# A hybrid decoder layer on one core: the inverse's last step with two heads side by side in the array, convolutions with two column places

## The chip, the cores and the metric

The kernel runs on one core of a Trainium2 chip, in one launch. The metric is the device time of one execution in microseconds (us), compared between kernels that ran on the same chip.

## What is computed

One layer of a decoder trunk for 512 tokens of width 1024, all in float32: a SwiGLU feed-forward block, a hybrid mixer, a second SwiGLU block, a last RMSNorm. The mixer projects its input into twelve groups of columns and has two branches. HGRN2 (8 heads) is a gated linear recurrence in chunks. Gated DeltaNet (16 value heads on 8 query/key heads) runs its q, k and v columns through a causal convolution of four taps with SiLU, and then, by chunks, the delta rule:

```python
def causal_short_conv(x, w):
    xp = jnp.pad(x, ((0, 0), (K - 1, 0), (0, 0)))
    return sum(xp[:, j:j + S] * w[j] for j in range(K))
...
    A = jnp.where(strict, jnp.einsum('bhntk,bhnsk->bhnts', kb, k) * Lmat, 0.0)
    T = lax.linalg.triangular_solve(eye + A, eye, left_side=True, lower=True, unit_diagonal=True)
    u = jnp.matmul(T, v * beta[..., None])
    w = jnp.matmul(T, kb * jnp.exp(gam)[..., None])
```

The inverse T of the unit lower triangular matrix is what the name "inverse" means below. The two branches are projected, gated, added and projected once more.

## The kernel before

Feature rows lie on the 128 partitions and the 512 tokens along the free dimension. Every large product is made of three matmuls (`mm3`, lines 164 to 166): weights and activations are split into a high and a low part in the type fp32r, and high by high, low by high and high by low are added up in PSUM. A weight block of 128x512 comes by DMA into a buffer `raw`, is cast by ScalarE (ACT) to `whi` and subtracted by VectorE (DVE) to `wlo` (lines 159 and 160 in the feed-forward blocks, 1368 and 1370 in the mixer). The program has three stages: the first feed-forward block, the mixer, and the second feed-forward block.

**What sets the order in the mixer.** Some hundred small generators (one for each head, inverse, convolution and gate) are run by a class `Desk` while the program is built. A generator asks for an engine and a time that the author priced (`yield V(512)` on DVE, `A(256)` on ACT, `T_(.9)` for .9 us of TensorE (PE)), for places (`yield "get", "mm", 1`), or for events. `Desk.run` keeps a clock for each engine, takes the request that can start first (ties by rank, or by a fourth element that goes ahead of the rank), and writes the instructions in that order. On the chip each engine then works through its own queue in order, and waits where an operand isn't there. So a change of a price or of a number of places moves instructions on all engines.

**Places the change speaks of.** `mm` is two PSUM banks for the large products: `product` (line 1376 on) takes one for a product of 24 matmuls with tile `pmm` (0.69 us for each three), or one for half of a product in token order with tile `pnat` (two token blocks, 48 matmuls). The bank goes back when the result has been read. `ta` is six buffers of 128x512 in SBUF (`TA = 6`), asked for by convolutions, the gates (`tgate`, tile `tg`, line 1136; `branch`, tile `yh`), the reloaded operands of the last product (`og`) and the merged gates (`mg`).

**A convolution** (`conv`, lines 763 to 785) waits for three `ta` places, reads the bank into `ci` on DVE (line 769; the bank is free after that), makes `cy` with one ACT and three DVE instructions (lines 774 and 777), a tanh `th` on ACT (line 780), and the output on DVE (line 783). Then it gives the three places back. 32 of them run, at most five unfinished at a time.

**The inverse** (`g_inv`, lines 940 to 987) runs eight times, each for eight 128x128 blocks: two heads by four token blocks, index s = 4i + c for head i. POOL has inverted the 32x32 diagonal blocks before. Two levels double them, 32 to 64 and 64 to 128; each level has two steps on PE with copies to SBUF on ACT:

```python
pe.matmul(q[a, s * hh:(s + 1) * hh], n2[b, s, a], ut[b, s, b], start=True, stop=True)
```

is the first (line 968, tile `pq`, copied into `acc`, line 971), and the second (line 978) multiplies by the transposed inverse (`tp` or `t64`) and is copied into `ut` (line 982). At the level 32 the rows `a` are two groups (0 to 31 and 64 to 95), so that two matmuls lie at different places of the array; at the level 64 there is one group, partitions 64 to 127 in and 0 to 63 out in the first step, and 0 to 63 in and out in the second: the eight blocks follow one another in one corner of the array. A float32 matmul is two recorded instructions: eight matmuls are "x16".

**The recurrence** (`g_rec`) uses the inverse: tiles `pw`, `pks`, `pog`, with DVE steps between (lines 1030 to 1070). `g_n` makes the 128x128 products ahead of it and takes a power on POOL (line 840).

Of the kernel before, what the change touches and what calls it, by code (L numbers as in the profile page):

```python
# [369 lines left out]
def mixer(tc, mp, e):  # L370
# [11 lines left out]
    def v3(ap, a):  # L382
        return ap.rearrange("p (a b) -> p a b", a=a)
# [378 lines left out]

    def conv(k, i, pt, out, n):

        yield "get", "ta", 3
        yield *V(512), 1
        ci = ta("ci", (P, T + 32))[:, :T + 3]
        dve.memset(ci[:, :3], 0.0)
        dve.tensor_tensor(ci[:, 3:], pt, rbc, op=ALU.mult)
        D.put("mm")  # L770
        wc = [cs[:, C_CV + 4 * i + j:C_CV + 4 * i + j + 1] for j in range(4)]
        yield A(512)
        y = ta("cy")
        act.activation(y, ci[:, :T], AF.Copy, scale=wc[0])
        for j in range(1, 4):
            yield V(550)
            dve.scalar_tensor_tensor(y, ci[:, j:j + T], wc[j], y, op0=ALU.mult, op1=ALU.add)
        yield A(512)
        th = ta("th")
        act.activation(th, y, AF.Tanh, scale=0.5)  # L780
        a, b = (v3(th, n), v3(y, n)) if n else (th, y)
        yield V(512)
        dve.scalar_tensor_tensor(out, a, 1.0, b, op0=ALU.add, op1=ALU.mult)
        D.put("ta", 3)
        D.fire(k)

    def g_e(u, st):
# [36 lines left out]
    def g_n(u, st):  # L824
        yield "on", "decays", ("k", u), *([("N", u - 1)] if u else []), *([("K", u - 4), ("R", u - 4)] if u > 3 else []), \
            ("kn", u) if u < 3 else "more"
        kq = st["kq"] = G["kq"][u % 4]
        kn = st["kn"] = G["kn"][u % 4]
        sm = st["sm"] = places["sm"]("sm", (P, 8, 8))
        for i in range(2):  # L830
            D.start((4, u, i), norms(u, i, kq, kn, sm))
        yield "on", ("norm", u, 0)

        hs = slice(2 * u, 2 * u + 2)
        rk = sm[:, 1, 0:4]
        yield V(4)
        dve.tensor_scalar(rk, sm[:, 0, 0:4], 4.0 * EPS, None, op0=ALU.add)
        yield "lag", EASE
        yield "use", "POOL", 1.2
        pool.tensor_tensor(rk, rk, mhalf[:, :4], op=ALU.pow)  # L840
        yield "lag", EASE
        s8 = lambda i: v3(sm[:, i], NT)
        c2, c3, c1 = st["c2"], st["c3"], st["c1"] = s8(2), s8(3), s8(4)
        yield "use", "DVE", .8
        dve.scalar_tensor_tensor(c2, beta[:, :, hs], 1.0, bc(rk, 2), op0=ALU.mult, op1=ALU.mult)
        dve.scalar_tensor_tensor(c3, c2, -1.0, bc(rk, 2), op0=ALU.mult, op1=ALU.mult)
        dve.tensor_tensor(c1, c3, eg[:, :, hs], op=ALU.mult)
        dve.tensor_scalar(c2, c2, 0.5, None, op0=ALU.mult)
        D.fire(("C", u))
        yield "on", ("q", u)  # L850
        yield "on", ("qm", 0), ("n2", u % 2)
        yield "get", "gm", 1
        gm, qm = places["gm"]("gm", (P, NT, P)), G["qm"][0]
        for hf in range(2):
            yield "get", "e", 1
            yield T_(.88)
            pq = ps("pgq", "e")
            for c in (2 * hf, 2 * hf + 1):
                pe.matmul(pq[:, (c % 2) * 256:(c % 2) * 256 + 256], kq[:, c, 0],
                          kq[:, c].rearrange("p a b -> p (a b)"), start=True, stop=True)  # L860
            p4 = pq.rearrange("p (c a b) -> p c a b", c=2, a=2)
            yield V(256)
            dve.tensor_tensor(gm[:, 2 * hf:2 * hf + 2], p4[:, :, 0], mid(strict, 2), op=ALU.mult)
            yield V(256)
            dve.tensor_tensor(qm[:, 2 * hf:2 * hf + 2], p4[:, :, 1], mid(tri, 2), op=ALU.mult)
            D.put("e")
        yield "on", ("E", u), *([("I", u - 2)] if u > 1 else [])
        st["at"] = []
        n2 = st["n2"] = G["n2"][u % 2]
        for i in range(2):  # L870
            a = G["at"][u % 4 * 2 + i]
            for c in range(NT):
                yield V(150)
                dve.scalar_tensor_tensor(n2[:, i, c], gm[:, c], c3[:, c, i:i + 1], a[:, c], op0=ALU.mult, op1=ALU.mult)
        D.put("gm")
        D.start((3, u), g_b(u, st))
        for i in range(2):
            a = G["at"][u % 4 * 2 + i]
            yield V(512)
            dve.tensor_tensor(a, qm, a, op=ALU.mult)  # L880
            st["at"].append(a)
        D.fire(("N", u))
# [57 lines left out]
    def g_inv(u, st):  # L940
# [10 lines left out]
        for b in range(4):  # L951
            r = slice(32 * b, 32 * b + 32)
            yield V(256)
            dve.transpose(ut[r, :, r], tp[r])
        for b in range(2):
            r = slice(32 * b, 32 * b + 32)
            yield A(256)
            act.copy(t64[r, :, r], tp[r])
        for hh in (32, 64):
            yield "get", "d", 1  # L960
            yield T_(.9)
            q = ps("pq1")
            qs = e["acc"]
            rows = [slice(2 * hh * g, 2 * hh * g + hh) for g in range(64 // hh)]
            nxt = [slice(2 * hh * g + hh, 2 * hh * g + 2 * hh) for g in range(64 // hh)]
            for s in range(8):
                for a, b in zip(rows, nxt):
                    pe.matmul(q[a, s * hh:(s + 1) * hh], n2[b, s, a], ut[b, s, b], start=True, stop=True)
            for a in rows:
                yield A(8 * hh)  # L970
                act.copy(qs[a, :8 * hh], q[a, :8 * hh])
            D.put("d")
            yield "get", "d", 1
            yield T_(.9)
            q2 = ps("pq2")
            for s in range(8):
                for a, b in zip(rows, nxt):
                    pe.matmul(q2[a, s * hh:(s + 1) * hh], tp[a, s] if hh == 32 else t64[:, s],
                              qs[a, s * hh:(s + 1) * hh], start=True, stop=True)
            for a, b in zip(rows, nxt):  # L980
                yield A(8 * hh)
                act.copy(ut[a, :, b], v3(q2[a, :8 * hh], 8))
            D.put("d")
            if hh == 32:
                yield V(256)
                dve.transpose(t64[32:64, :, 0:32], ut[0:32, :, 32:64])
        D.fire(("I", u))

    def g_rec(u, st):
# [175 lines left out]
    def operand(k, wait, get, make):  # L1165
# [9 lines left out]
        yield "lag", LAG["raw"]  # L1175
        if k > 8:
            yield "on", "projected"
        yield A(512)
        a, b = so[k] = make()
        act.copy(a, og)  # L1180
        yield V(512)
        dve.tensor_tensor(b, og, a.bitcast(F32), op=ALU.subtract)
        D.put("ta")
        D.fire(("so", k))
# [292 lines left out]
                                ("we", "we", 1, col), ("w", "w", 1, col)):  # L1477
        D.start((6, 0), claim(name, tag, n, shape))
    D.start((6, 0), claim("ut", "ut", 1, (P, 8, P), True))
    D.start((6, 0), claim("t64", "t64", 2, (64, 8, 64), True))  # L1480
    D.start((6, 0), second())
    D.start((6, 0), more())
    for u in range(8):
# [102 lines left out]
```

## Time and profile before

| | us |
|---|---|
| median of three runs | 1673.5 |
| the three runs | 1672.55, 1673.5, 1675.9 |
| the profiled execution | 1673.15 |
| its span, first to last instruction | 1671.4 |
| PE busy | 1645.5 |
| DVE busy | 968.0 |
| ACT busy | 698.0 |
| POOL busy | 322.4 |

The profiled execution took 1673.15 us by the same clock as the runs; 1.75 us of it lie outside the span. PE is busy nearly all the time. Matmuls are pipelined: one of 128x512 is recorded with some 0.39 us, and the next starts 0.23 us later, so that the distance between starts, not the recorded duration, is what an instruction costs on a full PE. In rows of the timeline the first column is the start, the second the duration of the merged group, the last the number of instructions; in square brackets stands the idle time before it and what ended it. PE's shapes are rows*columns of the array that the weights take, and then the moving operand.

### The profile page before, as it was taken

The page shows a single profiled execution, that of the slowest core. Times are in us where ns is not written, and L with a number is a line of the kernel's source. Part 1 is how long each engine was busy: PE and PEld are TensorE (multiplying, and loading weights), DVE is VectorE, ACT ScalarE, POOL GpSimd, SP SyncE. Part 2 cuts the span into 40 slices and gives each one's busy share as a digit, 9 for nine tenths or more (in the row PEclk, how much of TensorE's full clock was granted, in tenths as well). Part 3 has the DMA queues.
Part 4 walks back from the last instruction along what each step waited for, and adds up shares of the span by engine and source line. Part 5 has one row for each costly group of instructions (what it writes and reads, how often), then busy time and mean ns, then how long its engine had stood idle before and what let it go on. Part 6 is the DMA issues. An engine that isn't in the chain of part 4 may idle for free. (4 is left out here: it accounts for less than half of the span.)

```text
span 1671.4 us, 27476 instructions
## 1 busy us (share of the span) xinstructions
PE 1645.5 (98%) x10130; PEld 1397.4 (84%) x10130; DVE 968.0 (58%) x1992; ACT 698.0 (42%) x1523; POOL 322.4 (19%) x637
## 2 busy tenths in 40 slices
PE   8999999999999999999999999999999999999997
PEld 6888888888888898888888888887888888888886
DVE  5544443337677777657877788755545444444233
ACT  5333332333334345446665565554324433333332
POOL 2000000001121221561532756600001000000001
PEclk9999999999999999999999999999999999999998
DMA  5233333432222222444334353355544233333333
GB/s 174 89 98 98 95 98 108 117 119 71 77 65 66 77 82 73 148 136 108 99 112 117 95 131 106 118 159 166 174 145 138 89 96 100 95 98 95 98 94 112
DMA packets 141223, 181.21 MB, mean 108 GB/s; under 512 B 53008, under 2 KB 58640, under 8 KB 141088
## 3 DMA queue, kind: packets, MB, share of 16 engines
q1 hardware_dynamic: 140272, 177.78, 35.8%
q8 instruction: 80, 1.31, 0.3%
q0 software_dynamic: 384, 1.05, 0.2%
q10 hardware_dynamic: 432, 0.62, 0.1%
q14 instruction: 55, 0.45, 0.1%
HBM read 163.11 MB, written 16.29 MB: 107 GB/s over the span
## 5 line engine op out<-in xcount | busy, mean ns | idle before, releaser
L164 PE MATMUL pmm<-uh,whi 128*128 128x512 f32 (+1 forms) x1280 | 515.9, 403 | 7.9 <-ACT whi L301 7.0
L166 PE MATMUL pmm<-uh,wlo 128*128 128x512 f32 (+1 forms) x1280 | 500.0, 391 | 0.0
L165 PE MATMUL pmm<-ul,whi 128*128 128x512 f32 (+1 forms) x1280 | 499.8, 390 | 0.0
L159 ACT CAST whi<-raw 128x512 fp32r<-128x512 f32 (+1 forms) x290 | 176.5, 609 | 404.7 <-PE pmm L165 383.9
L160 DVE TENSOR_TENSOR wlo<-raw,whi 128x512 fp32r<-128x512 f32 (+1 forms) x290 | 203.1, 702 | 243.6 <-ACT whi L159 243.6
L164 PEld LDWEIGHTS pmm<-uh,whi 128*128 128x128 f32 (+1 forms) x1280 | 240.5, 188 | 56.4 <-ACT whi L301 7.3
L166 PEld LDWEIGHTS pmm<-uh,wlo 128*128 128x128 f32 (+1 forms) x1280 | 240.2, 188 | 52.6 <-DVE wlo L302 0.5
L165 PEld LDWEIGHTS pmm<-ul,whi 128*128 128x128 f32 (+1 forms) x1280 | 240.8, 188 | 45.3
L1368 ACT CAST whi<-raw 128x512 fp32r<-128x512 f32 x241 | 149.1, 620 | 250.0 <-PE pmm L165 163.3
L1370 DVE TENSOR_TENSOR wlo<-raw,whi 128x512 fp32r<-128x512 f32 x241 | 168.8, 702 | 140.0 <-ACT whi L1368 137.4
L202 POOL TENSOR_TENSOR acc<-acc,sqt 128x512 f32<-128x512 f32 x24 | 32.4, 1351 | 799.9 <-ACT sqt L200 799.6
L164 PE MATMUL pnat<-whi,uh 128*128 128x256 f32 x512 | 155.0, 303 | 3.2 <-DVE ggz L1157 2.0
L166 PE MATMUL pnat<-whi,ul 128*128 128x256 f32 x512 | 145.3, 284 | 0.0
L165 PE MATMUL pnat<-wlo,uh 128*128 128x256 f32 x512 | 145.2, 284 | 0.0
L164 PE MATMUL pmm<-gh,whi 128*128 128x512 f32 (+1 forms) x374 | 141.0, 377 | 0.0
L166 PE MATMUL pmm<-gh,wlo 128*128 128x512 f32 (+1 forms) x374 | 140.9, 377 | 0.0
L165 PE MATMUL pmm<-gl,whi 128*128 128x512 f32 (+1 forms) x374 | 140.8, 377 | 0.0
L910 POOL TENSOR_TENSOR fm<-gfs,ft 128x60 f32<-128x60 f32 (+24 forms) x248 | 94.9, 383 | 96.5 <-DMA ft<-hmask 77.9
L911 POOL TENSOR_TENSOR ft<-ft,fm 128x60 f32<-128x60 f32 (+24 forms) x248 | 99.6, 402 | 19.4
L164 PEld LDWEIGHTS pnat<-whi,uh 128*128 128x128 f32 x512 | 98.4, 192 | 5.8 <-DVE ggz L1157 2.2
L165 PEld LDWEIGHTS pnat<-wlo,uh 128*128 128x128 f32 x512 | 98.6, 193 | 0.7
L166 PEld LDWEIGHTS pnat<-whi,ul 128*128 128x128 f32 x512 | 98.2, 192 | 0.0
(374 smaller groups left out, 2189.0 us busy)
## 6 DMA issues: line engine op xcount, KB each, us to landing
raw<-wt SPq DMA_DIRECT2D x128, 256.0 KB
raw<-w1b SPq DMA_DIRECT2D x88, 256.0 KB
raw<-w1a SPq DMA_DIRECT2D x86, 256.0 KB
raw<-wn SPq DMA_DIRECT2D x64, 256.0 KB
raw<-w2b SPq DMA_DIRECT2D x45, 256.0 KB
raw<-w2a SPq DMA_DIRECT2D x40, 256.0 KB
raw<-wbg SPq DMA_DIRECT2D x32, 256.0 KB
gb<-gtd SPq DMA_DIRECT2D x16, 256.0 KB
```

The source lines that it names most:

```text
L159: act.copy(hi[:, :f], raw[:, :f])
L160: dve.tensor_tensor(lo[:, :f], raw[:, :f], hi[:, :f].bitcast(F32), op=ALU.subtract)
L164: pe.matmul(pt, ah, bh, start=first, stop=False)
L165: pe.matmul(pt, ah, bl, start=False, stop=False)
L166: pe.matmul(pt, al, bh, start=False, stop=last)
L202: pool.tensor_tensor(acc, acc, s, op=ALU.add)
L910: pool.tensor_tensor(tv, bc(m[:, j + 1:, j], w), t[:, j:j + 1, :w].to_broadcast([P, n, w]), op=ALU.mult)
L911: pool.tensor_tensor(t[:, j + 1:, :w], t[:, j + 1:, :w], tv, op=ALU.add)
L1368: act.copy(hi, raw)
L1370: dve.tensor_tensor(lo, raw, hi.bitcast(F32), op=ALU.subtract)
```

## The change

The level 32 is written out as before (`level32`), with the price of a PE step at .65 instead of .9. At the level 64 (`level64`), the four blocks of the second head are put into the other half of the array's columns: the first step reads partitions 64 to 127 for all blocks and writes partitions 0 to 63 of `q` for the first head and 64 to 127 for the second; its copy to `acc` is one of 128x256 in place of one of 64x512. For the second step `t64` holds the second head on partitions 64 to 127 (shape 128x4x64 in place of 64x8x64), so each head has its own corner of the array; the result goes to `ut` in two copies of 64x256 in place of one of 64x512. The matmuls alternate between the heads. The price of a step is .6 instead of .9. To fill `t64`, ACT has four copies of 32x128 where there were two of 32x256, and DVE two transposes of 32x128 where there was one of 32x256. The two levels' matmuls are as many and as large as before.

A convolution asks for two `ta` places: its tanh is written over `ci`. Three further edits change ranks alone: the power on POOL (line 840), and the cast and the subtraction of a reloaded operand (`operand`, lines 1178 to 1182), go ahead of others that could start at the same time.

```diff
--- before.py
+++ after.py
@@ -762,7 +762,7 @@
 
     def conv(k, i, pt, out, n):
 
-        yield "get", "ta", 3
+        yield "get", "ta", 2
         yield *V(512), 1
         ci = ta("ci", (P, T + 32))[:, :T + 3]
         dve.memset(ci[:, :3], 0.0)
@@ -776,12 +776,12 @@
             yield V(550)
             dve.scalar_tensor_tensor(y, ci[:, j:j + T], wc[j], y, op0=ALU.mult, op1=ALU.add)
         yield A(512)
-        th = ta("th")
+        th = ci[:, :T]
         act.activation(th, y, AF.Tanh, scale=0.5)
         a, b = (v3(th, n), v3(y, n)) if n else (th, y)
         yield V(512)
         dve.scalar_tensor_tensor(out, a, 1.0, b, op0=ALU.add, op1=ALU.mult)
-        D.put("ta", 3)
+        D.put("ta", 2)
         D.fire(k)
 
     def g_e(u, st):
@@ -836,7 +836,7 @@
         yield V(4)
         dve.tensor_scalar(rk, sm[:, 0, 0:4], 4.0 * EPS, None, op0=ALU.add)
         yield "lag", EASE
-        yield "use", "POOL", 1.2
+        yield "use", "POOL", 1.2, 1
         pool.tensor_tensor(rk, rk, mhalf[:, :4], op=ALU.pow)
         yield "lag", EASE
         s8 = lambda i: v3(sm[:, i], NT)
@@ -952,38 +952,64 @@
             r = slice(32 * b, 32 * b + 32)
             yield V(256)
             dve.transpose(ut[r, :, r], tp[r])
+
         for b in range(2):
             r = slice(32 * b, 32 * b + 32)
-            yield A(256)
-            act.copy(t64[r, :, r], tp[r])
-        for hh in (32, 64):
+            for i in range(2):
+                yield A(128)
+                act.copy(t64[64 * i + 32 * b:64 * i + 32 * b + 32, :, r], tp[r, 4 * i:4 * i + 4])
+        qs = e["acc"]
+        lo, hi = slice(0, 64), slice(64, 128)
+
+        def level32():
+            rows, nxt = (slice(0, 32), slice(64, 96)), (slice(32, 64), slice(96, 128))
             yield "get", "d", 1
-            yield T_(.9)
+            yield T_(.65)
             q = ps("pq1")
-            qs = e["acc"]
-            rows = [slice(2 * hh * g, 2 * hh * g + hh) for g in range(64 // hh)]
-            nxt = [slice(2 * hh * g + hh, 2 * hh * g + 2 * hh) for g in range(64 // hh)]
             for s in range(8):
                 for a, b in zip(rows, nxt):
-                    pe.matmul(q[a, s * hh:(s + 1) * hh], n2[b, s, a], ut[b, s, b], start=True, stop=True)
+                    pe.matmul(q[a, s * 32:(s + 1) * 32], n2[b, s, a], ut[b, s, b], start=True, stop=True)
             for a in rows:
-                yield A(8 * hh)
-                act.copy(qs[a, :8 * hh], q[a, :8 * hh])
+                yield A(256)
+                act.copy(qs[a, :256], q[a, :256])
             D.put("d")
             yield "get", "d", 1
-            yield T_(.9)
+            yield T_(.65)
             q2 = ps("pq2")
             for s in range(8):
                 for a, b in zip(rows, nxt):
-                    pe.matmul(q2[a, s * hh:(s + 1) * hh], tp[a, s] if hh == 32 else t64[:, s],
-                              qs[a, s * hh:(s + 1) * hh], start=True, stop=True)
+                    pe.matmul(q2[a, s * 32:(s + 1) * 32], tp[a, s], qs[a, s * 32:(s + 1) * 32], start=True, stop=True)
             for a, b in zip(rows, nxt):
-                yield A(8 * hh)
-                act.copy(ut[a, :, b], v3(q2[a, :8 * hh], 8))
+                yield A(256)
+                act.copy(ut[a, :, b], v3(q2[a, :256], 8))
             D.put("d")
-            if hh == 32:
-                yield V(256)
-                dve.transpose(t64[32:64, :, 0:32], ut[0:32, :, 32:64])
+
+        def level64():
+
+            heads = [(4 * i + j, slice(64 * i, 64 * i + 64), slice(64 * j, 64 * j + 64)) for j in range(4) for i in range(2)]
+            yield "get", "d", 1
+            yield T_(.6)
+            q = ps("pq3")
+            for s, r, c in heads:
+                pe.matmul(q[r, c], n2[hi, s, lo], ut[hi, s, hi], start=True, stop=True)
+            yield A(256)
+            act.copy(qs[:, :256], q[:, :256])
+            D.put("d")
+            yield "get", "d", 1
+            yield T_(.6)
+            q2 = ps("pq4")
+            for s, r, c in heads:
+                pe.matmul(q2[r, c], t64[r, s % 4], qs[r, c], start=True, stop=True)
+            for i in range(2):
+                yield A(256)
+                act.copy(ut[lo, 4 * i:4 * i + 4, hi], v3(q2[64 * i:64 * i + 64, :256], 4))
+            D.put("d")
+
+        yield from level32()
+        for i in range(2):
+            yield V(128)
+            dve.transpose(t64[64 * i + 32:64 * i + 64, :, 0:32], ut[0:32, 4 * i:4 * i + 4, 32:64])
+        yield from level64()
         D.fire(("I", u))
 
     def g_rec(u, st):
@@ -1175,10 +1201,10 @@
         yield "lag", LAG["raw"]
         if k > 8:
             yield "on", "projected"
-        yield A(512)
+        yield *A(512), 1
         a, b = so[k] = make()
         act.copy(a, og)
-        yield V(512)
+        yield *V(512), 1
         dve.tensor_tensor(b, og, a.bitcast(F32), op=ALU.subtract)
         D.put("ta")
         D.fire(("so", k))
@@ -1477,7 +1503,7 @@
                                 ("we", "we", 1, col), ("w", "w", 1, col)):
         D.start((6, 0), claim(name, tag, n, shape))
     D.start((6, 0), claim("ut", "ut", 1, (P, 8, P), True))
-    D.start((6, 0), claim("t64", "t64", 2, (64, 8, 64), True))
+    D.start((6, 0), claim("t64", "t64", 2, (P, 4, 64), True))
     D.start((6, 0), second())
     D.start((6, 0), more())
     for u in range(8):
```

## The prediction

> **What bounds the kernel now.** I read the page first, then PE by stages, then the list of what PE waited for, and last the timeline around the places that the change touches. The page gives the span and the share of each engine:
>
> ```profile
> span 1671.4 us, 27476 instructions
> PE 1645.5 (98%) x10130; PEld 1397.4 (84%) x10130; DVE 968.0 (58%) x1992; ACT 698.0 (42%) x1523; POOL 322.4 (19%) x637
> ```
>
> PE is the bound, and no other engine comes near. The four stretches below are most of the first feed-forward block, the mixer up to the first place where the changed order differs, the rest of the mixer up to its last product, and what follows; the columns are the length and the busy time of PE, PEld, DVE, ACT and POOL, the granted clock, and the DMA.
>
> ```profile
> 20.00:355.00 335.00, 334.03 (x1485) 276.60 (x1485) 151.60 (x228) 116.73 (x192) 12.36 (x10) 1.00 0.34 102
> 355.00:649.00 294.00, 294.00 (x2891) 258.12 (x2890) 206.47 (x539) 113.98 (x265) 56.50 (x70) 1.00 0.26 79
> 649.00:1170.00 521.00, 513.59 (x3462) 442.99 (x3461) 378.79 (x867) 287.81 (x774) 226.97 (x530) 1.00 0.43 122
> 1170.00:1660.00 490.00, 488.79 (x2240) 408.06 (x2239) 216.56 (x336) 165.88 (x271) 18.85 (x17) 1.00 0.36 109
> ```
>
> All that the change can reach lies in the third row. There PE is idle for 521.00 - 513.59 = 7.4 us; DVE and ACT have more than 140 us to spare. So two things count: how long PE's own instructions take, and which of the 7.4 us of waits stay. The waits of that stretch, by what ended them (total, times, longest):
>
> ```profile
> PE pmm L164 <- DVE tg L1136: 2.3, 1, 2.3
> PE pnat L164 <- DVE ggz L1157: 2.0, 1, 2.0
> PE pnat L164 <- DVE ci L769: 1.2, 1, 1.2
> PE pks L1030 <- DVE s L1070: 1.1, 2, 0.6
> PE pw L1043 <- DVE gx L1034: 0.5, 1, 0.5
> PE ptv L934 <- DVE gqm L865: 0.3, 1, 0.3
> ```
>
> They add up to 7.4: the list is whole.
>
> **Part 1: the last step's matmuls, two heads at a time.** The timeline of PE around the first inverse: each step with the row that follows it.
>
> ```profile
> 728.70 0.69 PE L968 MATMUL pq<-gut,gn 32*32 32x32 f32 x32
> 729.32 0.50 PE L164 MATMUL pmm<-uh,whi 128*128 128x512 f32 x1
> ...
> 735.83 1.14 PE L968 MATMUL pq<-gut,gn 64*64 64x64 f32 x16
> 736.90 0.65 PE L813 MATMUL ptk<-sq,h 128*128 128x128 f32 x4
> ...
> 738.88 1.14 PE L978 MATMUL pq<-acc,gt 64*64 64x64 f32 x16
> 739.96 0.50 PE L164 MATMUL pmm<-uh,whi 128*128 128x512 f32 x1
> ```
>
> From its start to the next one's, a 64-wide step takes 1.07 and 1.08 us for 16 instructions in one corner; the 32-wide step takes 0.62 us for 32 instructions at two places of the array. Does work at two places run side by side? The HGRN2 heads show it apart from the width, in products over all 128 rows that land on one, two or four groups of columns (lines 648 and 634):
>
> ```profile
> 413.62 0.45 PE L648 MATMUL pl<-qp,ke 128*32 128x32 f32 x16
> 414.00 0.39 PE L164 MATMUL pnat<-whi,uh 128*128 128x256 f32 x1
> ...
> 416.70 0.68 PE L648 MATMUL pl<-qp,ke 128*64 128x64 f32 x8
> 417.31 0.39 PE L164 MATMUL pnat<-whi,uh 128*128 128x256 f32 x1
> ...
> 418.94 0.45 PE L634 MATMUL pl<-qp,ke 128*32 128x16 f32 x32
> 419.31 0.39 PE L164 MATMUL pnat<-whi,uh 128*128 128x256 f32 x1
> ```
>
> 32 instructions on four groups take 0.37 us and 16 on two groups 0.38: eight to each group in both. 16 to each group (the 32-wide step) take 0.62. So the time goes by the instructions of one group, and the groups run beside each other. Of 64-wide ones, eight in one group take 417.31 - 416.70 = 0.61 us. The changed step has eight in each of two groups: I take 0.61. Each inverse saves (1.07 - 0.61) + (1.08 - 0.61) = 0.93, and eight inverses **7.4 us**, all of it on the bound engine. Ends: nothing, if the two halves follow one another; and no more than 7.4, since no row shows eight such instructions in less.
>
> [...] Line 648 at 413.62 has all rows in common and still takes 0.38 for 16. [...]
>
> The copies around the steps change on ACT:
>
> ```order
> L1368 CAST whi<-raw 128x512
> L971 COPY acc<-pq_7490 64x512
> L816 COPY gkn<-ptk 128x512
> L820 ACTIVATE ptk,sm<-ptk 128x128 x4
> L982 COPY gut<-pq_7527 64x8x64
> ```
>
> That was ACT at the 64 level of the first inverse before; this is the same place in the changed kernel:
>
> ```order
> L1394 CAST whi<-raw 128x512
> L820 ACTIVATE ptk,sm<-ptk 128x128
> L996 COPY acc<-pq_7578 128x256
> L820 ACTIVATE ptk,sm<-ptk 128x128 x2
> L801 ACTIVATE gqm<-gb,gx 128x128 x2
> L1005 COPY gut<-pq_7607 64x4x64 x2
> ```
>
> The copy between the two steps has half the elements to a partition, the one behind them has become two. The copies of this kind before, shortest, median and longest in ns (32x256 at the low end, 64x512 at the high end):
>
> ```profile
> L971 ACT COPY acc<-pq x24: 343/364/583, 729.4 to 1112.2; 32x256 f32<-32x256 f32 x16, 64x512 f32<-64x512 f32 x8
> ```
>
> By it an inverse pays .36 for .58 ahead of the second step, 2 x .36 for .58 behind it, and two more short copies for `t64`, at most .36 each: at the worst +0.6 us on ACT, and two DVE transposes for one. ACT is free for 521.00 - 287.81 us, and PE has large products between the steps, so I take 0. Without that cover a late copy would hold PE by its own .36, at most 2.9 us for eight inverses.
>
> **Part 2: the banks that convolutions held.** The longest stall of the stretch is at 662.71:
>
> ```profile
> 653.73 0.39 PE L166 MATMUL pmm<-uh,wlo 128*128 128x512 f32 x1
> ...
> 660.45 0.28 PE L166 MATMUL pnat<-whi,ul 128*128 128x256 f32 x1
> 662.71 0.52 PE L164 MATMUL pnat<-whi,uh 128*128 128x256 f32 x1 [1.98 <-DVE ggz L1157]
> ```
>
> ```profile
> 665.88 0.68 DVE L769 TENSOR_TENSOR ci<-pmm,rbc 128x512 f32<-128x512 f32 x1
> ```
>
> A convolution's product is complete at 653.73, but DVE reads it only at 665.88: for 12 us one of the two banks is held, and the halves of the next product (`pnat`) share the other. PE has to wait until the gate (line 1157) has emptied it. Why so late stands in DVE's order, from the gates of the waiting product (`pnat_6536`) to that convolution (`pmm_6433`), before:
>
> ```order
> L1157 SCALAR_TENSOR_TENSOR ggz_5781<-thg_6613,pnat_6536 128x256
> L874 SCALAR_TENSOR_TENSOR gn2_5718<-gm_6501,sm_6308,gat_5542 128x128
> L1157 SCALAR_TENSOR_TENSOR ggz_5781<-thg_6618,pnat_6536 128x256
> L732 TENSOR_TENSOR hrho_6514<-hrho_6514,rcol_83 128x4
> L735 SCALAR_TENSOR_TENSOR hon_6515<-po_6385,hrho_6514,hg_5780 128x128 x4
> L874 SCALAR_TENSOR_TENSOR gn2_5718<-gm_6501,sm_6308,gat_5542 128x128
> L880 TENSOR_TENSOR gat_5541<-gqm_6386,gat_5541 128x512
> L880 TENSOR_TENSOR gat_5542<-gqm_6386,gat_5542 128x512
> L783 SCALAR_TENSOR_TENSOR h_70<-th_6573,cy_6450 128x4x128
> L768 MEMSET ci_6691 128x3
> L769 TENSOR_TENSOR ci_6691<-pmm_6433,rbc_74 128x512
> ```
>
> The read comes right behind line 783, with which an older convolution gives its three places back: two convolutions had all six. Now the same product is `pmm_6435`, and the gates are those of `pnat_6529`:
>
> ```order
> L777 SCALAR_TENSOR_TENSOR cy_6451<-ci_6356,cs_75,cy_6451 128x512
> L768 MEMSET ci_6536 128x3
> L769 TENSOR_TENSOR ci_6536<-pmm_6435,rbc_74 128x512
> L1396 TENSOR_TENSOR wlo_6526<-raw_6398,whi_6527 128x512
> L777 SCALAR_TENSOR_TENSOR cy_6451<-ci_6356,cs_75,cy_6451 128x512
> L777 SCALAR_TENSOR_TENSOR cy_6458<-ci_6432,cs_75,cy_6458 128x512
> L863 TENSOR_TENSOR gm_6509<-pgq_6555,sq_76 128x256
> L865 TENSOR_TENSOR gqm_6385<-pgq_6555,sq_76 128x256
> L783 SCALAR_TENSOR_TENSOR h_70<-ci_6356,cy_6451 128x4x128
> L777 SCALAR_TENSOR_TENSOR cy_6458<-ci_6432,cs_75,cy_6458 128x512 x2
> L732 TENSOR_TENSOR hrho_6468<-hrho_6468,rcol_83 128x4
> L735 SCALAR_TENSOR_TENSOR hon_6469<-po_6384,hrho_6468,hg_5780 128x128 x4
> ```
>
> Three convolutions are under way (`cy_6451`, `cy_6458` and the new `ci_6536`), and the bank is read ahead of everything that it stood behind. So the 1.98 us should go. They had a sequel, by the granted clock (the last figure but two):
>
> ```profile
> 660.00:665.00 5.00, 3.02 (x18) 2.81 (x17) 3.44 (x12) 2.74 (x7) 0.00 (x0) 0.78 0.01 3
> 665.00:670.00 5.00, 5.00 (x39) 5.00 (x39) 2.16 (x5) 1.76 (x4) 0.52 (x1) 0.88 0.17 28
> ```
>
> The clock was not full for a while after the wait: (0.22 + 0.12) x 5.00 = 1.7 us of PE's work were lost. It goes if the wait goes. The second stall of the kind is named after the convolution itself:
>
> ```profile
> 994.90 0.39 PE L164 MATMUL pnat<-whi,uh 128*128 128x256 f32 x1 [1.25 <-DVE ci L769]
> ```
>
> In the changed order convolutions' reads follow their products closely there too. Together 1.98 + 1.7 + 1.25 = **4.9 us**. Ends: nothing, if waits as long come up at other places of the new order; and 4.9 + 4.2 = 9.1 if the other waits of the list go as well (2.3 + 1.1 + 0.5 + 0.3 = 4.2).
>
> **Part 3: what is only moved.** The other waits, 4.2 us, I keep as they are. The recurrence's (lines 1030 and 1043) come from a chain of PE and DVE that the change doesn't shorten. The last,
>
> ```profile
> 1165.62 0.47 PE L164 MATMUL pmm<-sogb,whi 128*128 128x512 f32 x1 [2.26 <-DVE tg L1136]
> ```
>
> is a gate that gets a `ta` place late, after the last convolution; gates, reloaded operands and merged gates ask for as many places as before. The tanh over `ci` adds no wait: it needs `cy`, which the last reading of `ci` makes. The power's rank moves it in POOL's queue, among the solver's instructions of the 32x32 blocks; POOL is busy for 226.97 of 521.00 us, so I take 0. An inverse that came late would show as a wait of the recurrence, whose largest one here is 0.6. The number of DMAs stays, the SP queue issues them in another order, and the large products keep their number. In PE's order the runs of large products between other work are 248 before and 248 now, so no more switches between kinds of matmul are paid.
>
> **Sum.** 1673.15 - 7.4 - 4.9 = 1660.8 for an execution like the profiled one, which lies 0.35 below the median of the runs shown. I say **1661**; its own range is 1658 to 1664, by the 4.2 us of other waits going either way by some two thirds.
>
> **Rivals.**
>
> *The waits move.* 32 convolutions, 16 gates and eight inverses stand in another order, planned with prices. For it: the waits of before were in no plan either. Against: the two that I take away have one cause, which the order shows gone. Then only part 1 is left: 1673.15 - 7.4 = 1665.8.
>
> *One step of the two stays serial.* Part 1 gives 3.7: 1664.5. If both do, the change doesn't do what it says, and part 2 alone gives 1668.2. Against both: 0.37 us for 32 on four groups. For: no row has 64-wide halves.
>
> *All waits go*, since the steps' prices (.65 and .6) are now near what a step costs (0.62 and 0.61; before .9 against 0.62 and 1.07), so that the plan drifts less: 1673.15 - 7.4 - 9.1 = 1656.7.
>
> *Slower: convolutions crowd the gates out.* With three convolutions in six places nothing is left for a gate (`tg` or `yh`, 24 of them), whose product then holds a bank as the convolution did. One such hold costs what the one at 662.71 did, 1.98 + 1.7 = 3.7 us. To be slower than before by 0.2% (3.3 us, about what a measurement of this kernel can tell from no change) it takes 12.3 + 3.3 = 15.6 us, so it decides from the fifth hold on: 1660.8 + 5 x 3.7 = 1679.3. For it: the wait at 1165.62 is of this sort. Against: a gate needs one place where a convolution needs two at once.
>
> **How the numbers follow.** Forecast 0.55; the waits move 0.17; one step serial 0.09; both serial 0.04; all waits go 0.05; slower 0.08; within 0.2%, by part 1 or 2 and some new waits, 0.02. Faster by over 0.2%: 0.55 + 0.17 + 0.09 + 0.04 + 0.05 = 0.90. The range from 1656 to 1668 takes in all but both serial and what is slower or equal, 0.14.
>
> **What would show it.** [...] Part 2: no wait of PE for line 769 or for the gates of `pnat` (now line 1183) near 650 to 670, and a granted clock of 1.00 there. Part 3: PE's idle time from 649 to the end of the mixer, near 4.2. The prediction is wrong if that idle time is 7 or more, or if the steps keep their length.

## The result: no change that the measurement can tell

| | before | after |
|---|---|---|
| median of 20 runs each on one chip, us | 1674.35 | 1674.09 |
| lowest and highest | 1671.69 to 1675.9 | 1669.64 to 1677.36 |
| ratio, 95% interval | | 0.9999 [0.9992, 1.0005] |
| the profiled execution, us | 1673.15 | 1671.58 |
| its span, us | 1671.4 | 1669.8 |

The forecast was 1661 with a range from 1656 to 1668: the time lies above all of it. Of the three parts of the reasoning the first two hold as mechanisms, and the profile after shows it. The page first:

```profile
span 1669.8 us, 27534 instructions
PE 1640.4 (98%) x10130; PEld 1392.4 (83%) x10130; DVE 969.9 (58%) x2000; ACT 699.3 (42%) x1547; POOL 322.1 (19%) x637
```

PE's share is 98% as before, and its busy time is 5 us less. The steps of the first inverse at the level 64, each with the row behind it:

```profile
748.82 0.68 PE L994 MATMUL pq<-gut,gn 64*64 64x64 f32 x16
749.43 0.50 PE L164 MATMUL pmm<-uh,whi 128*128 128x512 f32 x1
...
751.02 0.68 PE L1002 MATMUL pq<-acc,gt 64*64 64x64 f32 x16
751.63 0.50 PE L164 MATMUL pmm<-uh,whi 128*128 128x512 f32 x1
```

From start to start both steps take 0.61 us, and so do all sixteen. **Part 1 came to the hundredth of a microsecond.** Next the stretch of the two held banks, and then the mixer as a whole, by stretches with the granted clock as the last figure but two:

```profile
660.00:665.00 5.00, 5.00 (x45) 5.00 (x44) 3.30 (x9) 3.79 (x9) 0.31 (x1) 1.00 0.01 3
665.00:670.00 5.00, 5.00 (x30) 4.39 (x29) 4.48 (x10) 2.89 (x6) 0.00 (x0) 1.00 0.49 152
```

```profile
649.00:1168.00 519.00, 508.20 (x3463) 437.56 (x3462) 381.39 (x874) 289.46 (x799) 226.49 (x530) 0.99 0.42 123
```

From 660 to 670 PE is now busy throughout at full clock: **part 2's waits went.** But over the mixer PE is idle for 519.00 - 508.20 = 10.8 us, where before it was 7.4 and the prediction had 4.2. What it waits for there (total, times, longest):

```profile
PE pq L971 <- DVE gut L954: 5.2, 2, 4.6
PE pmm L164 <- DVE tg L1162: 2.4, 1, 2.4
PE pog L1083 <- DVE x L1074: 1.7, 1, 1.7
PE pq L981 <- ACT acc L974: 1.5, 1, 1.5
```

No wait of this list names a convolution (line 769) or the gates of `pnat` (line 1183). Three of its four names were not on the list of before; the fourth, `tg`, was the last wait there. The largest one stands at the first inverse, at 736.78. On PE:

```profile
731.84 0.39 PE L166 MATMUL pmm<-uh,wlo 128*128 128x512 f32 x1
736.78 0.24 PE L971 MATMUL pq<-gut,gn 32*32 32x32 f32 x2 [4.56 <-DVE gut L954]
```

The product before it is finished, and the next instruction in PE's order is the inverse's. Its matmuls need the second and the fourth of four transposes of DVE (line 954). DVE:

```profile
729.53 0.43 DVE L954 STREAM_TRANSPOSE gut<-gtp 32x256 f32<-32x256 f32 x1
735.57 0.69 DVE L1396 TENSOR_TENSOR wlo<-raw,whi 128x512 fp32r<-128x512 f32 x1 [5.61 <-ACT whi L1394]
736.29 1.36 DVE L954 STREAM_TRANSPOSE gut<-gtp 32x256 f32<-32x256 f32 x3
```

One transpose is done at 729.53, the other three stand behind a subtraction for a large product, which waits 5.61 us for its cast on ACT. ACT:

```profile
726.88 0.62 ACT L1394 CAST whi<-raw 128x512 fp32r<-128x512 f32 x1 [2.99 <-DMA raw<-wt]
733.09 1.28 ACT L801 ACTIVATE x<-gb,gx 128x128 f32<-128x128 f32 x4 [5.59 <-DMA gb<-gtd]
...
734.94 0.60 ACT L1394 CAST whi<-raw 128x512 fp32r<-128x512 f32 x1
```

The cast stands behind four activations of another head, which wait 5.59 us for `gb`, a row of gates that a DMA spreads over all partitions (line 796). And SP, which issues the DMAs:

```profile
721.18 5.87 SPq L923 DMA_DIRECT2D gln<-nt  x4
727.14 0.51 SPq L1377 DMA_DIRECT2D raw<-wt  x1
727.76 0.38 SPq L1151 DMA_DIRECT2D md<-yh  x1
728.18 0.42 SPq L796 DMA_DIRECT2D gb<-gtd  x1
```

The load of `gb` is issued only at 728.18, behind four loads of the solver's results (`gln`) that hold SP for 5.87 us. So PE's 4.56 us come down a chain of four queues: SP, ACT, DVE, PE. In the kernel before no load of `gb` stood between 715 and 737, and DVE made all four transposes in one go:

```profile
726.44 1.81 DVE L954 STREAM_TRANSPOSE gut<-gtp 32x256 f32<-32x256 f32 x4
```

The wait at the mixer's end has the same form. SP issues the store of a gate, `td<-tg`, behind nine loads for the gates' merging, 4.8 us after the tanh that makes it was done (1142.11 on ACT), and DVE can't write the next `tg` into the place until that store is done; the product whose bank DVE is to read then stops PE:

```profile
1146.94 0.32 SPq L1151 DMA_DIRECT2D td<-tg  x1
```

```profile
1152.58 0.69 DVE L1162 TENSOR_TENSOR tg<-pmm,rbc 128x512 f32<-128x512 f32 x1 [5.64 <-DMA td<-tg]
```

```profile
1153.42 0.54 PE L164 MATMUL pmm<-uh,whi 128*128 128x512 f32 x1 [2.36 <-DVE tg L1162]
```

Both waits were followed by a stretch at half clock:

```profile
737.26:744.10 6.84, 6.40 (x42) 4.72 (x42) 6.14 (x11) 4.81 (x12) 5.94 (x12) 0.50 0.39 116
1153.68:1157.10 3.42, 3.42 (x9) 2.68 (x9) 3.30 (x8) 1.59 (x4) 0.00 (x0) 0.50 0.37 115
```

PE is busy in them for 6.40 + 3.42 = 9.8 us and does about half as much (its 128x512 matmuls start 0.43 us apart there, 0.23 elsewhere): some 4.9 us are lost, against 1.7 before. The ledger of the span: 7.4 saved by the steps; 10.8 - 7.4 = 3.4 more of waits; 4.9 - 1.7 = 3.2 more lost to the clock. That is -0.8; the span moved by -1.6.

### The profile page after: what moved, and what is told of

Read it like the earlier page. It is cut to its first block, busy times and chain, and to the rows that moved or that the text cites. A ratio compares the mean times of both kernels' runs of the same rounds, so it can differ in the third digit from the quotient of the medians.

```text
span 1669.8 us, 27534 instructions
## 1 busy us (share of the span) xinstructions
PE 1640.4 (98%) x10130; PEld 1392.4 (83%) x10130; DVE 969.9 (58%) x2000; ACT 699.3 (42%) x1547; POOL 322.1 (19%) x637
## 5 line engine op out<-in xcount | busy, mean ns | idle before, releaser
L164 PE MATMUL pmm<-uh,whi 128*128 128x512 f32 (+1 forms) x1280 | 516.4, 404 | 10.2 <-ACT whi L301 6.9
L911 POOL TENSOR_TENSOR ft<-ft,fm 128x60 f32<-128x60 f32 (+24 forms) x248 | 99.3, 400 | 19.4
```

The source lines that it names most:

```text
L164: pe.matmul(pt, ah, bh, start=first, stop=False)
L911: pool.tensor_tensor(t[:, j + 1:, :w], t[:, j + 1:, :w], tv, op=ALU.add)
```

## The experiments

The theory after the two profiles: the steps save their 7.4 us, and the new order, which prices, places and ranks set together, gives them back in waits and in the slow clock behind them, above all through SP's queue. The rivals: the shorter steps aren't paid, because PE then waits for what it had met in time before, in any order; or one edit does it by itself, the two places or the ranks. The letters in the texts on record are those of each text.

Eleven kernels ran, in three groups; in each group the kernel before ran on the same chip (1674.71 us for experiments 1 to 4, 1675.08 for 5 to 8, 1675.0 for 9 to 11). All compute the whole layer.

**1. Only the new steps.** Before's order, prices, ranks and three places; only the level 64 is placed as in the change, in the same place of the order.

```diff
-                pe.matmul(q[a, s * hh:(s + 1) * hh], n2[b, s, a], ut[b, s, b], start=True, stop=True)
+                for s, r, c in heads:
+                    pe.matmul(q[r, c], n2[hi, s, lo], ut[hi, s, hi], start=True, stop=True)
...
+                    pe.matmul(q2[r, c], t64[r, s % 4], qs[r, c], start=True, stop=True)
```

> Part 1 alone: the order, the prices and the three places of the kernel before are kept, row by row on PE; only the 64 level's placement, its copies and the transposes are the changed kernel's. Theory A (the matmuls' saving is real and the new order gives it back in waits): 16 steps save 0.46 us each and the waits stay at the 7.4 us of before, so 1674.4 - 7.4 = 1667.0, ratio 0.9956. Rival B (the saving doesn't reach the end because something else than PE paces the mixer): 1674, ratio 1.000.

Measured: 1670.94 us, ratio 0.9983 [0.9975, 0.9991], between the two numbers of the text. Its steps take 0.61 us too, so 7.4 us left PE's work; 3.8 of them arrived by the medians, 2.8 by the ratio. In the profiled run PE's waits in the mixer grew from 7.4 to 11.6 us, though PE's instructions stand in the same order, one for one. One example, in the kernel before:

```profile
968.94 0.41 DVE L865 TENSOR_TENSOR gqm<-pgq,sq 128x256 f32<-128x256 f32 x1
```

```profile
969.72 0.81 PE L859 MATMUL pgq<-h 128*128 128x256 f32 x3
```

and in this kernel:

```profile
968.17 0.41 DVE L865 TENSOR_TENSOR gqm<-pgq,sq 128x256 f32<-128x256 f32 x1
```

```profile
968.73 0.89 PE L859 MATMUL pgq<-h 128*128 128x256 f32 x3 [1.73 <-DVE gqm L865]
```

Line 865 empties the tile that PE's next instruction writes. Before, DVE was done with it just before PE came (968.94 + 0.41 = 969.35 against 969.72). PE now comes earlier, DVE by only 0.77 us, and PE waits 1.73. DVE has hardly a gap there: the "140 us to spare" of the prediction are a mean over the mixer, and here it is DVE's queue that ends last. So a saving on PE is paid out only where the other engines are ahead by more than the saving.

**2. Only two places for a convolution.**

```diff
-        yield "get", "ta", 3
+        yield "get", "ta", 2
...
-        th = ta("th")
+        th = ci[:, :T]
...
-        D.put("ta", 3)
+        D.put("ta", 2)
```

> Part 2 alone: the kernel before with two places to a convolution and the tanh over ci, all else as it was; the order is planned anew. Theory A as in the prediction (the waits at 662 and 994 go, nothing else comes): 1674.4 - 4.9 = 1669.5, ratio 0.997. Theory A with new waits, as the changed kernel has them: between 1670 and 1678, and the wait for line 769 is gone all the same. Rival B: 1674, ratio 1.000.

Measured: 1689.9 us, ratio 1.0097 [1.0084, 1.011]: the edit that part 2 valued at -4.9 costs 15 us by itself. All three times of the text missed; that the waits for line 769 go was right. Its waits:

```profile
PE pto L1103 <- DVE on L1095: 9.5, 1, 9.5
PE pq L968 <- DVE gut L954: 4.5, 2, 3.9
...
PE ptk L813 <- DVE h L783: 0.8, 1, 0.8
...
```

No bank is held any more: lines 769, 1157 and 1136 are all gone from the list. Two other waits have come. One is the chain of the four queues (3.9 at 736). The other stands at the mixer's end: the large products have moved ahead, so none is left to put beside the last head's recurrence, and PE waits 9.5 us for line 1095. On DVE that line stands behind three merges of gates (line 1210) that wait for their operands: the power that it needs is ready on POOL at 1184.24, and it starts at 1189.60. The last of the merges:

```profile
1188.99 0.69 DVE L1210 SCALAR_TENSOR_TENSOR mi<-mt,mi 128x512 f32<-128x512 f32 x1 [1.24 <-DMA mt<-td]
```

and SP issues the loads of these operands only behind four weight blocks that hold it for 11 us:

```profile
1168.62 11.15 SPq L1358 DMA_DIRECT2D raw<-wbg  x4
1179.83 0.42 SPq L1201 DMA_DIRECT2D mi<-md  x1
```

**3. The new order with the old steps.** The changed kernel; its level 64 works in one corner again, and the prices, places and ranks of the change stay.

```diff
...
-            heads = [(4 * i + j, slice(64 * i, 64 * i + 64), slice(64 * j, 64 * j + 64)) for j in range(4) for i in range(2)]
+            heads = [(s, lo, slice(64 * s, 64 * s + 64)) for s in range(8)]
...
```

> The order, the prices and the places of the changed kernel are kept row by row on PE; the 64 level's matmuls lie in one corner of the array as before, with one copy of 64x512 between the steps. Theory A: 16 steps take 0.46 us longer, 1674.1 + 7.4 = 1681.5, ratio to before 1.0043, less where a longer step shortens a wait (the 4.6 us one at 736 comes ahead of the first 64 level, so it stays). Rival B: 1674, ratio 1.000.

Measured: 1682.02 us, ratio 1.0046 [1.0034, 1.0058]. With experiment 1 this makes a square of four, by the ratios: the new steps bring 1.0046 - 0.9999 = 0.47% or 7.9 us in the new order and 0.17% or 2.8 us in the old one; the new order costs 0.46% or 7.7 us with the old steps and 0.16% or 2.7 us with the new ones. So the steps pay, and the new order eats it.

**4. The load of `gb` out of SP's queue.** The changed kernel with one word changed: ACT issues it.

```diff
-            sp.dma_start(gb, gtd[hd_:hd_ + 1].rearrange("o (c b) -> o c b", c=NT).to_broadcast([P, NT, P]))
+            act.dma_start(gb, gtd[hd_:hd_ + 1].rearrange("o (c b) -> o c b", c=NT).to_broadcast([P, NT, P]))
```

> The changed kernel, with the 16 loads of gb issued by ACT and not by SP; nothing else is moved on PE, DVE or POOL. Theory A1 (the 4.6 us wait at 736 comes from a gb load that stands behind the solver's results in the SP queue and holds ACT, DVE and PE in turn): the waits of 4.6 and 0.7 us go with the slow clock behind them (about 2), 1674.1 - 7 = 1667, ratio to before 0.9957. Rival A2 (the solver's result itself is late, and PE would wait for it anyway): the wait stays at 4 to 5 us and the time at 1674, ratio 1.000.

Measured: 1669.81 us, ratio 0.9975 [0.9966, 0.9985], between the text's 1667 and 1674. PE's order is that of the change. Its waits:

```profile
PE pmm L164 <- DVE tg L1162: 2.3, 1, 2.3
PE pog L1083 <- DVE x L1074: 1.9, 1, 1.9
PE pq L971 <- DVE gut L954: 1.6, 3, 0.7
...
```

The wait at 736 is two of 0.68 in place of 4.56 and 0.68:

```profile
733.66 0.24 PE L971 MATMUL pq<-gut,gn 32*32 32x32 f32 x2 [0.68 <-DVE gut L954]
734.58 0.69 PE L971 MATMUL pq<-gut,gn 32*32 32x32 f32 x30 [0.68 <-DVE gut L954]
```

ACT issues the load at 724.54, where SP did at 728.18, and waits 1.19 us for `gb`, not 5.59:

```profile
729.88 1.28 ACT L801 ACTIVATE x<-gb,gx 128x128 f32<-128x128 f32 x4 [1.19 <-DMA gb<-gtd]
```

This shows that the chain SP, ACT, DVE, PE is the cause of most of that wait. The gain is 4.3 us by the medians, 4.0 by the ratios, and not theory A1's 7: the two waits of 0.68 us stay, 3.4 us at half clock still follow them, and so do 3.4 us behind the wait for line 1074, which grew from 1.71 to 1.92.

**5. The gates' stores out of SP's queue as well.** Experiment 4, and `keep` issues the stores `td<-tg` from ACT.

```diff
...
-        D.start((6, i), keep(td[i], g, "ta", ("t", i)))
+        D.start((6, i), keep(td[i], g, "ta", ("t", i), act))
```

> The changed kernel with the loads of gb and the gates' stores (td) issued by ACT; same rows on PE, DVE and POOL. Theory A1, carried on: the wait of 2.3 us near 1153 for line 1162 comes from a store that stands in the SP queue behind weight loads, so it shrinks to 1 us or less and the slow clock behind it goes: 1669.8 (gb alone) - 1.5 to 3 = 1667 to 1668, ratio to before 0.996. Rival (the store's own landing is what the gate waits for): the wait stays above 2 us, 1669.8, ratio 0.9975.

Measured: 1666.17 us (1664.85 to 1668.26), ratio 0.9951 [0.9939, 0.9964]. **This beats both kernels**, the one before by 8.9 us and the changed one by 7.9 (by the ratios, which compare on one chip, by 8.2 and 8.0). It lies a little below the text's 1667 to 1668. Of its waits:

```profile
PE pq L981 <- ACT acc L974: 1.5, 1, 1.5
...
PE pmm L164 <- DVE tg L1162: 0.8, 1, 0.8
PE pq L971 <- DVE gut L954: 0.7, 1, 0.7
...
```

The store that held `tg` is issued 0.6 us after its tanh (1140.42 and 1141.02), not 4.8. The wait for `tg` fell from 2.4 to 0.8, that for `gut` from 5.2 to 0.7, and the mixer's idle time is 7.4 us, no more than before the change; only then does part 1's saving arrive in full (1675.08 - 7.4 = 1667.7).

**6. Without the edits of ranks.** The changed kernel with the ranks of before at line 839 and in `operand`.

```diff
-        yield "use", "POOL", 1.2, 1
+        yield "use", "POOL", 1.2
...
-        yield *A(512), 1
+        yield A(512)
...
-        yield *V(512), 1
+        yield V(512)
```

> The changed kernel without its three edits of ranks (the power on POOL, the cast and the subtraction of a reloaded operand); planned anew. In the kernel with two places alone PE waits 9.5 us for the last head and then two more times. Theory C (the ranks are what keeps the last head from coming late): a wait of 8 us or more near the end of the mixer, time 1674 + 10 to 16, ratio 1.006 to 1.010. Rival D (the new prices of the steps do it): no wait above 3 us there, time within 1670 to 1678, ratio 0.998 to 1.002.

Measured: 1672.5 us, ratio 0.9984 [0.9975, 0.9993], 2.6 us faster than before. The wait at 736 is still there (5.33 us), and the mixer ends with short waits, 2.0 for line 1121 and 1.6 in two pieces behind it. Theory C fell, and rival D's numbers came true. The rank edits gain nothing that this shows, and the wait at 736 doesn't come from them. That the prices of the steps keep the last head in time, as D has it, is not shown: no run changes the prices alone.

**7 and 8. Another plan, not one instruction changed.** `SLACK` is the time by which the planner takes every request for PE, except the large products', as later than it is, so that products go first. It is 0.9 in place of 0.8, in the changed kernel and in the kernel before.

```diff
-SLACK = 0.8
+SLACK = 0.9
```

> The changed kernel with one number of the planner altered (the lead that PE's small products are given, 0.8 to 0.9): the same instructions, in another order. Theory A (the waits are those of the particular order, and each order draws others): the waits of 4.6, 1.5 and 1.7 us are not at the same places, PE's idle time in the mixer is anywhere from 5 to 20 us, and the time between 1668 and 1684. Rival E (the waits belong to the change, whatever the order): the same waits within 0.5 us, and 1674.

> The kernel before with the same number altered (0.8 to 0.9). Theory A: other waits than before, time between 1671 and 1686; with the run of the changed kernel under the same number it shows how far a plan moves the time with no instruction changed. Rival E: 1674 within 1.

Measured: the changed kernel 1674.13 us, ratio 0.9995 [0.9986, 1.0004]; the kernel before 1693.85, ratio 1.0116 [1.0102, 1.0131]. The same instructions of before in another order take 19 us more, which is past theory A's range (it ended at 1686). The changed kernel's waits are as many in this plan (10.8 us), but others: none at 736, and 3.1 at the mixer's end.

**9. The queue edits in the kernel before.** `gb` and `td` are issued by ACT, as in experiment 5.

> The kernel before; only the loads of gb (line 796) and the stores of the gates td (line 1125) are issued by ACT and not by SP. Theory A (the loads behind SP's queue cost time only in the changed order, where they are issued late behind the gln loads): before has no wait at 736, and of its 7.4 us of waits only the 2.26 at 1165 hangs on td; at most 1.5 us go: ratio 0.999 to 1.000. Theory B (the two edits are worth the same 7.9 us in any order): 1675 - 7.9 = 1667, ratio 0.995.

Measured: 1674.97 us, ratio 1.0005 [0.9996, 1.0014]: nothing, as theory A had it. The edits are worth 7.9 us in the changed order and nothing in the old one. Before has no wait behind a load of `gb`, and the wait for `tg` near 1165 stays (2.15 us for 2.26): in that order SP issued the store 0.3 us after its tanh (1160.96 and 1161.30), so there was little to gain.

**10. The changed kernel with three places again.** Experiment 2's diff the other way round.

> The changed kernel, but convolutions ask for three places again (their tanh has a place of its own); new steps, prices and ranks stay. Theory A (a place number is one more draw of the plan: it takes away the waits of the held banks and brings others): a wait of PE for line 769 or for a gate comes back, the wait at 736 may go or stay, and the time lies between 1666 and 1682, ratio 0.994 to 1.004. Theory B (two places cost about 15 us by themselves, as they did alone in the old order): without them 1659, ratio 0.991.

Measured: 1694.58 us, ratio 1.0121 [1.0107, 1.0134]. Both texts missed: theory A's range ended at 1682, and B had the wrong sign. The waits:

```profile
...
PE pnat L164 <- DVE tg L1162: 3.7, 1, 3.7
PE pmm L164 <- DVE ci L769: 3.6, 1, 3.6
PE pmm L164 <- DVE tg L1162: 2.5, 2, 2.3
...
PE pnat L164 <- DVE x L1183: 2.0, 1, 2.0
PE pnat L164 <- DVE ggz L1183: 2.0, 1, 2.0
PE pnat L164 <- DVE ci L769: 1.0, 1, 1.0
...
```

These six rows, for lines 769, 1162 and 1183, name readers of a product's bank: 3.7 + 3.6 + 2.5 + 2.0 + 2.0 + 1.0 = 14.8 of 24.0 us. In the changed kernel 2.4 of that sort is left. So part 2's mechanism is larger than I took it for in this order (the two places are worth 20 us), while in the old order the same edit costs 15: what it is worth can't be told apart from the order that it leads to.

**11. Experiment 1 with the queue edits.**

> The kernel before with the new placement of the 64-wide steps alone (before's order, prices and three places), and with the loads of gb and the stores of td issued by ACT. Theory A (what the shorter steps uncovered in that order are waits for DVE's queue at 823 and 969, not for SP's): they stay, only the wait near 1162 shrinks by 1.5 us: 1669.5, ratio 0.9965 to 0.9985. Theory B (the uncovered waits hang on SP's queue as well): the 4.2 us that the step alone had not brought come back, 1667, ratio 0.9955 or less.

Measured: 1674.97 us, ratio 0.9996 [0.9986, 1.0006] (one run of 3317.13 us, twice the others, is not in the ratio). Both texts missed: the queue edits brought nothing here, and the 4 us of experiment 1 are gone as well. Its waits are those of experiment 1, among them 2.05 us in place of 1.46 for line 865 at 825, and 2.32 for `tg`, which did not shrink. What differs most is the clock: two stretches of 3.4 us at half clock follow the waits at 663 and 1165; the profiled run of experiment 1 has none. Over all runs it is less: the mean granted clock is 0.9956 here and 0.9962 in experiment 1, by estimate 1.0 us of the 2.2 between the two ratios. Moving the stores did not help the wait for `tg` here, for the reason seen in experiment 9: the old order's store does not stand behind other loads (in experiment 1 SP issues it at 1157.60, 0.3 us after its tanh).

## Where each kernel's time went

For each profiled run: its span, PE's waits of over 0.2 us from 640 to 1210, and what the clock took there (an estimate: half of PE's busy time in the stretches at half clock, as 128x512 matmuls start 0.43 us apart there and 0.23 elsewhere). The last column is the span less both.

| kernel | span | waits | lost to the clock | both | rest |
|---|---|---|---|---|---|
| *old steps* | | | | | |
| before | 1671.4 | 7.4 | 1.7 | 9.1 | 1662.3 |
| 9: before, queue edits | 1673.0 | 8.5 | 1.7 | 10.2 | 1662.8 |
| 3: new order | 1680.6 | 12.3 | 7.1 | 19.4 | 1661.2 |
| 2: two places alone | 1687.6 | 16.9 | 8.1 | 25.0 | 1662.5 |
| 8: before, other plan | 1689.6 | 20.7 | 5.5 | 26.2 | 1663.4 |
| *new steps* | | | | | |
| 5: after, both queue edits | 1663.8 | 7.4 | 1.7 | 9.1 | 1654.7 |
| 1: old order | 1667.7 | 11.6 | 0.0 | 11.6 | 1656.1 |
| 4: after, `gb` from ACT | 1667.4 | 8.6 | 3.4 | 12.0 | 1655.4 |
| after | 1669.8 | 10.8 | 4.9 | 15.7 | 1654.1 |
| 11: old order, queue edits | 1672.8 | 12.6 | 3.4 | 16.0 | 1656.8 |
| 7: after, other plan | 1672.4 | 10.8 | 6.0 | 16.8 | 1655.6 |
| 6: after, old ranks | 1672.6 | 11.1 | 6.3 | 17.4 | 1655.2 |
| 10: after, three places | 1690.6 | 24.0 | 12.0 | 36.0 | 1654.6 |

The rest is 1661.2 to 1663.4 with the old steps (mean 1662.4) and 1654.1 to 1656.8 with the new ones (mean 1655.3): 7.1 us apart, near part 1's 7.4, whatever the order. All else is waits and clock, and these differ from plan to plan. The clock's part also differs from run to run: the kernel before has a granted clock of 0.995 to 0.997 over its runs, and 0.001 of 1671.4 is 1.7 us, while the table has one run of each kernel. Of the thirteen kernels the one before is lowest, with experiment 5; the middle one has 16.0 us.

## Why the prediction was wrong

**Part 1 was right**: 0.61 us a step, in both steps (rows at 748.82 and 751.02), in all eight inverses, and the rest column shows the sum. The rival of a step that stays serial fell: no run shows its 3.7, and the means of the rest column are 7.1 apart.

**Part 2 was right as a mechanism**: the banks are read in time, and the 1.98, its 1.7 us of clock and the 1.25 are gone. As a term of the sum it fails. The -4.9 were the price of the waits that leave; the edit also sets a new order, and experiments 2 and 10 give the edit +15 and -20 us in two orders.

**The step that failed is part 3**: "The other waits, 4.2 us, I keep as they are", and the nothing that stood for "the SP queue issues them in another order". The new order brought 10.8 us of waits in place of 4.2, and 4.9 us of slow clock in place of none: 6.6 + 4.9 = 11.5 us, against the 10.8 by which the profiled run missed the sum (1671.58 - 1660.8); the other 0.7 lies within the scatter of the rest column. So the sign of being wrong that the prediction named, 7 us or more of idle time, was there. The two largest waits, 4.56 and 2.36 us with the slow stretches behind them, come from SP's queue, which I named and didn't follow past SP: experiments 4 and 5 take most of them away and get 7.9 us back. That chain can be read in the order alone: a load of `gb` behind four `gln`, a cast behind the activations that need `gb`, the transposes behind the subtraction that needs the cast. The 4.8 us by which experiment 5's profiled run (1665.58) still misses the sum are 7.4 - 4.2 = 3.2 of waits and 1.7 of clock; no run takes these apart.

**Two smaller errors.** I took it that an inverse that came late would show in the recurrence; it showed in the inverse's own first step, which PE has in its order right behind a product. And I counted a saving on PE in full because DVE and ACT are idle for 140 us and more of the mixer; experiment 1 has PE reach DVE's queue at 823 and 969, and half of the saving arrives by the medians (3.8 of 7.4), less by the ratio (2.8).

**The rivals.** "The waits move" was right in kind, and too small at 1665.8: its bound let waits only replace the two that went. Nothing capped them there, as the table shows. The rival of gates crowded out of their places fell: of the waits after only the 2.36 for `tg` is of that sort, and it was there before. That all waits go fell with the 10.8 us.

## What to carry to other kernels

Where a change makes a planner write another order, price the order and not only the edit: the kernel before is one draw with few waits, and other draws of nearly the same work had up to 27 us more of waits and slow clock (36.0 against 9.1). Follow each moved DMA down the queues, from the engine that issues it to the one that waits for its data, and to what stands behind that one in order, until PE is reached or an engine with slack at that very place. And add to a long wait on a busy PE the slow clock behind it: here all 15 waits of 2.36 us or more in the mixer were followed by it or lay in it, and eight of the 17 between 1.87 and 2.35 us were followed by it.

## What the runs showed of the hardware

**The clock after a wait.** In all traces of this case the granted clock in the mixer is 1.00 or 0.50, and stretches at 0.50 last 3.4 us (before, 662.80 to 666.20; after, 1153.68 to 1157.10), 6.8 (after, 737.26 to 744.10) and 10.2 (experiment 10, 1006.2 to 1016.4). They begin 1.9 to 5.0 us after PE's idle time began (2.1 at 663 in the kernel before; 5.0 and 2.6 in the changed one). Of PE's waits in the mixer in the thirteen profiled runs, all 15 of 2.36 us or more were followed by such a stretch (or lay in one); of 17 between 1.87 and 2.35 us eight were, eight were not, and one (1.97) was only after further short waits; of the shorter ones outside such a stretch none was, save two pairs close together (1.39 and 0.42 us in experiment 5, 0.68 and 0.68 in experiment 4). The same wait of 1.98 us at 663 was followed by 3.4 us at half clock in four kernels (before, from 662.80, is one) and by none in experiment 1.

**Halves of the columns.** Four 64-wide float32 matmuls, that is eight instructions, in each of two halves of the columns take 0.61 us together (after, rows at 748.82 and 751.02), where all sixteen instructions in one corner took 1.07 and 1.08 (before, rows at 735.83 and 738.88), whether both halves read the same rows (line 994) or different ones (line 1002); both write one tile, `pq`.

**After a change of the kind of matmul.** In the kernel before, the first 128x512 matmul behind the 32-wide step starts at 729.32 and the next one 0.34 us later, not 0.23.
